# Elementwise work of the projections from GpSimd to VectorE, and layer 1's first in-projection spread over the whole second output stage

## The chip, the cores and the metric

The kernel runs on one core of a Trainium2 chip. The metric is device time in microseconds (us), lower is better. The kernel before takes 3068.93 us, the median of three runs (3067.5 to 3072.47). Engines go by the profile's names: PE is TensorE's matmul, PEld its weight load, DVE is VectorE, ACT is ScalarE, POOL is GpSimd, SP is SyncE, which issues all DMAs here.

## The reference, cut to what matters

A decoder trunk of two layers over 1040 tokens of width 1024 (16 meta tokens in front of 1024), in float32:

```python
for layer in range(2):
    hn = rmsnorm(h, norm_mix_w[layer])
    hq,hf,hi,hg, gq,gk,gv,gz, ga,gb, su = split(hn @ w_in[layer])   # 1024 x 3336
    y_a = hgrn2_mixer(hq, hf, hi, hg, ...)      # 4 heads of 64, chunked recurrence
    y_b = gdn_mixer(gq, gk, gv, gz, ga, gb, ...)  # conv + silu, 4 heads of 128, triangular solve per chunk, state
    y_c = s5_mixer(su, ...)                     # 16 groups, linear state space, gelu, gate
    h = h + concat(y_a, y_b, y_c) @ w_out[layer]      # 1024 x 1024
    hn = rmsnorm(h, norm_mlp_w[layer])
    h = h + square(relu(hn @ w1[layer])) @ w2[layer]  # 1024 x 4096 x 1024
return rmsnorm(h, final_norm_w)[:, 16:]
```

The recurrences carry a state from one token chunk to the next.

## The kernel before

The 1040 tokens are two blocks of 520, b = 0 and 1, with the width on the partitions (eight tiles of 128 x 520). For each layer and block there are three parts: the in-projection (`projection`), the recurrences over the block (`states`), and the output stage (`out_mlp`: w_out, norm, MLP).

**Weights.** Every product with w_in, w_out, w1 or w2 is done in split precision: the operand x as xh + xl, the weight as wh + wl, three matmuls for each. A weight tile is a "granule" of 128 x 512 (four 128 x 128 pieces): SP loads it to `wr`, ACT makes the high part `wh` (line 459), and the low part `wl` is a tensor_tensor at line 113, called from `split`. There are three buffers each of wr, wh and wl (N_W). A granule feeds 24 matmuls of 260 to 264 columns, or 12 of 512. A product with w_in, w_out or w1 takes two granules, one with w2 takes one. Products go to two PSUM buffers `pd`; DVE takes them out.

**In-projection.** 26 products with w_in and a narrow one, in this order: S5's inputs, rows of gates (`in_rows`), convolutions for the delta-net heads with SiLU (`in_conv`, `silu`), between them the decay matrices (`gdn_decay`), a triangular solve (`gdn_solve`), in block 0 the tables of S5 (`s5_layer`), more convolutions, gates (`in_gate`), and the two pairs of HGRN heads (`in_hgrn`, then `hgrn`: many small matmuls in `mxh`, exponentials, products).

**States.** `states` runs the delta-net windows (ten items, each a chain of a dozen steps, the state `GS` handed on from window to window) beside S5. Their matmuls write `mxt`, and each item ends in a DMA at line 1043 that stores its outputs `ydr`. The output stage of a block reads all of that block's ydr first.

**Order.** `run` writes: in-projection and states of (layer 0, b 0), the same of (0, 1), output stage of (0, 0); then layer 1's first in-projection interleaved with output stage (0, 1); then states (1, 0); then the rest of output stage (0, 1); in-projection and states of (1, 1); output stages (1, 0) and (1, 1). In the interleaved part each piece of the projection allows so many units of the output stage, one unit being one granule's product: DENSE after a product, MIX after a step of decay or HGRN. A list scheduler then orders the instructions of each engine, weights ahead of the rest; what is written late can stand early on an engine, but within one engine the order is fixed when the program runs.

Lines 107, 110, 113, 116, 121 and 125 are helpers, so in the profile tile names tell the work apart: `pd` products, `s` rows of 520 in the projection, `h` the residual, `uh`/`ul` the MLP's hidden operand, `mh`/`nh`/`qh` projection scratch, `mt`/`nt` states scratch.

Of the kernel before, what the change touches and what calls it, by code (L numbers as in the profile page):

```python
# [94 lines left out]
class Kern:  # L95
# [91 lines left out]
    def setup(self):  # L187

        nc = self.nc
        self.take(T)  # L190
        self.K, self.XD, self.SC, self.grp = {}, None, None, "h"
        warm = self.n([128, 2, 128])
        nc.vector.memset(warm, 0.0)
        for _ in range(7):
            self.mm(self.mps()[:, :256], warm[:, 0], warm.rearrange("p a b -> p (a b)"))
        self.ident = self.load_const("ident", [128, 128])
        nc.scalar.preload_act_table_set("natural_log_exp_and_others")
# [269 lines left out]
    def granule_now(self, fill, keep):  # L467
        raw = self.tl(self.big, [128, 4, 128], "wr", N_W)
        fill(raw)
        if keep:  # L470
            lo, hi = [self.operand(tag)[:, :512].rearrange("p (k m) -> p k m", k=4) for tag in ("xl", "xh")]
        else:
            lo = self.tl(self.big, [128, 4, 128], "wl", N_W, F32R)
            hi = self.tl(self.big, [128, 4, 128], "wh", N_W, F32R)
        self.split(raw, hi, lo, self.nc.gpsimd)
        return hi, lo

    def weights(self, ap):
# [30 lines left out]
    def normed_rows(self, h, wcol, b, spare=None):  # L509

        nc = self.nc
        xs = [], []
        acc = self.s()
        for k in range(KD):
            self.square(acc, h[k], k)
        self.squares, self.r = acc, None
        r = self.scale()
        if b == 0:
            self.hist = self.tl(self.big, [128, KD, HIST], "hist", 1)
        for k in range(KD):  # L520
            w = self.prm[:, wcol + k:wcol + k + 1]
            xn = self.tl(self.sp, [128, T + 8], "s", N_S)[:, :T + HIST]
            if b == 0:
                nc.gpsimd.memset(xn[:, :HIST], 0.0)
            else:
                nc.gpsimd.tensor_copy(xn[:, :HIST], self.hist[:, k])
            self.stt(xn[:, HIST:], h[k], w, r, ALU.mult, ALU.mult)
            if b == 0:
                nc.gpsimd.tensor_copy(self.hist[:, k], xn[:, T:])
            hi, lo = (next(spare), next(spare)) if spare else (self.operand("xh"), self.operand("xl"))  # L530
            nc.scalar.copy(hi, xn)
            self.tt(lo, xn, hi.bitcast(F32), ALU.subtract)
            xs[0].append(hi)
            xs[1].append(lo)
        return xs
# [45 lines left out]

    def silu(self, n, out):
        self.sigma(out, n)
        self.tt(out, out, n, ALU.mult, eng=self.nc.gpsimd)

    def cols(self, l, col, xs, runs=None):
        wts = self.ready.pop((l, col), None) or self.in_weights(l, col)
# [5 lines left out]
    def cols_ab(self, l, xs):  # L593


        nc = self.nc
        wi = self.ins["w_in"][l].rearrange("(g k p) m -> g p k m", k=4, p=128)
        ps = self.tl(self.pd, [128, 2, 512], "pd", 2)
        for g in range(2):
            raw = self.tl(self.big, [128, 4, 128], "wr", N_W)[:, :, :8]  # L600
            w = self.tl(self.big, [128, 4, 128], "wh", N_W, F32R)
            nc.sync.dma_start(raw, wi[g][:, :, C_GA:C_GA + 8])
            nc.scalar.copy(w[:, :, 0:32].rearrange("p k (r m) -> p k r m", r=4), raw.unsqueeze(2).to_broadcast([128, 4, 4, 8]))
            self.tt(w[:, :, 32:40], raw, w[:, :, 0:8].bitcast(F32), ALU.subtract, eng=nc.gpsimd)
            for k in range(4 * g, 4 * g + 4):
                for c in range(2):
                    cs = slice(HIST + c * HN, HIST + (c + 1) * HN)
                    self.mm(ps[0:40, c, :HN], w[:, k % 4, 0:40], xs[0][k][:, cs], start=(k == 0), stop=False)
                    self.mm(ps[0:40, c, :HN], w[:, k % 4, 0:40], xs[1][k][:, cs], start=False, stop=(k == KD - 1))
        return ps  # L610
# [118 lines left out]
    def projection(self, l, b, xs, hook=None, first=False):  # L729


        DENSE, MIX = 2, 0.5
        self.Y = self.YS[b] = self.tl(self.dr, [KD, 128, T], "ydr", 2)
        if first:
            self.setup_mixers()
        g = {"z": self.tl(self.dr, [6, 128, T], "gated", 2)}
        us = self.in_s5(l, xs)
        yield 2 * DENSE
        g["rows"] = self.in_rows(l, b, xs)
        yield MIX  # L740
        g["qkv"] = self.QKV = self.tl(self.dr, [12, 128, T], "qkvd", 2)
        self.gdn_begin(l, b, g)
        for p in range(2):
            for i in (2 * p, 2 * p + 1, 4 + 2 * p, 5 + 2 * p):
                self.in_conv(l, b, xs, i)
                yield DENSE
            for _ in pipeline([self.gdn_decay(g, w, p) for w in range(NW)], GAP_DECAY):
                yield MIX
        self.gdn_solve()
        self.gdn_scales()  # L750
        if b == 0:
            self.s5_layer(l)
        if hook:
            trace(hook)
        for i in range(8, 12):
            self.in_conv(l, b, xs, i)
            yield DENSE
        for i in range(4):
            self.in_gate(l, xs, C_GZ + 128 * i, g["z"][i])
            yield DENSE  # L760
        for j in range(2):
            hd = self.in_hgrn(l, xs, j)
            yield 3 * DENSE
            self.in_gate(l, xs, C_HG + 128 * j, g["z"][4 + j])
            yield DENSE
            for _ in self.hgrn(l, b, j, hd, g["z"][4 + j]):
                yield MIX
        self.mixed = g, us
# [82 lines left out]
    def gdn_decay(self, g, w, pair):  # L851
# [23 lines left out]
        self.act(ln, ln, AF.Ln, bias=EPS)  # L875
        self.act(b2, ln, AF.Exp, scale=-1.0)
        MA = self.m()[:W, :4 * W].rearrange("p (a b c) -> p a b c", a=2, b=2)
        self.tt(MA, E.unsqueeze(1).to_broadcast([W, 2, 2, W]), K["tri"].unsqueeze(2).to_broadcast([W, 2, 2, W]), ALU.mult, eng=nc.gpsimd)
        self.tt(b2, b2, self.gsc[:, w, 1, hs], ALU.mult)
        yield  # L880
        self.tt(MA[:, 0], MA[:, 0], b2.unsqueeze(2).to_broadcast([W, 2, W]), ALU.mult, eng=nc.gpsimd)
        self.tt(MA, pg, MA, ALU.mult)
        yield
        nc.sync.dma_start(self.item(self.MAd, it), MA)
# [15 lines left out]
    def gdn_solve(self):  # L900
# [20 lines left out]
        low = lambda t: t[:, H:, 0:H]  # L921
        mid = self.n([80, H, H])
        for dst, a, bt in ((mid, low(Dg), Tm[:, 0:H, 0:H]), (low(Tm), Tm[:, H:, H:], mid)):
            for n, i0 in enumerate(range(0, H, 3)):
                k = min(3, H - i0)
                prod = tmp()[:, :k * H * H].rearrange("p (i c j) -> p i c j", i=k, c=H)
                self.tt(prod, bt.rearrange("p j c -> p c j").unsqueeze(1).to_broadcast([80, k, H, H]),
                        a[:, i0:i0 + k, :].unsqueeze(2).to_broadcast([80, k, H, H]), ALU.mult, eng=nc.gpsimd if n % 2 else None)
                nc.vector.tensor_reduce(dst[:, i0:i0 + k, :], prod, mybir.AxisListType.X, ALU.add)
        Tt = Dg  # L930
        nc.scalar.copy(Tt, Tm.rearrange("p a b -> p b a"))
# [373 lines left out]
    def out_mlp(self, l, b, h, last=False):  # L1305
# [10 lines left out]
        for m in range(KD):  # L1316
            ps = self.product(self.weights(self.ins["w_out"][l][:, 128 * m:128 * m + 128]), xs)
            self.tt(self.half(h[m]), self.half(h[m]), ps, ALU.add)
            yield 2
        xs = self.normed(h, 16 + 8 * l)  # L1320
        NG = D_FF // 512
        hid = {}
# [140 lines left out]
    def run(self):  # L1463
        self.setup()
        self.H, self.YS = {}, {}
        nxt = {}

        def early():

            nxt[1] = self.htiles()  # L1470
            yield from self.load_x(1, nxt[1])
            self.save_h(1, nxt[1])
        h = self.htiles()
        trace(self.load_x(0, h))
        self.ready = {(0, col): self.in_weights(0, col) for col in (C_SU, C_SU + 128)}
        self.setup_norms()
        self.block(0, 0, h, early(), True)
        self.block(0, 1, nxt[1])
        h = self.get_h(0)
        trace(self.out_mlp(0, 0, h))  # L1480
        xs = self.normed_rows(h, 8, 0, self.spare_operands())
        self.save_h(0, h)

        h = self.get_h(1)
        rest = self.out_mlp(0, 1, h)
        due = 0
        for n in self.projection(1, 0, xs):
            due += n
            while due > 0:
                due -= next(rest, 1e6)  # L1490
        self.states(1, 0)
        trace(rest)
        self.save_h(1, h)
        self.block(1, 1, h)
        for b in range(NB):

            self.take(512 if b == 0 else T)
            h = self.get_h(b)
            self.steps = None
            trace(self.out_mlp(1, b, h, b == 1))  # L1500
            self.finish(b, h, self.steps)


# [27 lines left out]
```

## Time and profile before

| | |
|---|---|
| median of three runs | 3068.93 us |
| the profiled execution's own time, its span | 3072.88 us, 3071.1 us |
| mean granted TensorE clock | 0.954 of 2.4 GHz |
| busy, share of the span | PE 93%, PEld 87%, DVE 51%, ACT 42%, POOL 51% |
| chain that ended last, by engine | PE 68%, DVE 13%, DMA 5% |

The stretches in which the rows below are cut follow the issue of each part's first weights: 26 to 264 us is the in-projection of (0, 0); 264 to 568 that of (0, 1) with states (0, 0); 568 to 1132 output stage (0, 0); 1132 to 1894 output stage (0, 1), with layer 1's first in-projection up to about 1645 and states (1, 0) behind it; 1894 to 2106 the in-projection of (1, 1); 2106 to 2613 output stage (1, 0) with states (1, 1); then output stage (1, 1). What overlaps is cut by its start.

A busy time is a union of spans. PE counts as busy also while it works at the lower of its two clock levels, 1.2 GHz, so a stretch's clock is to be read beside it.

### The profile page before, as it was taken

The page shows a single profiled execution, that of the slowest core. Times are in us where ns is not written, and L with a number is a line of the kernel's source. Part 1 is how long each engine was busy: PE and PEld are TensorE (multiplying, and loading weights), DVE is VectorE, ACT ScalarE, POOL GpSimd, SP SyncE. Part 2 cuts the span into 40 slices and gives each one's busy share as a digit, 9 for nine tenths or more (in the row PEclk, how much of TensorE's full clock was granted, in tenths as well). Part 3 has the DMA queues.
Part 4 walks back from the last instruction along what each step waited for, and adds up shares of the span by engine and source line. Part 5 has one row for each costly group of instructions (what it writes and reads, how often), then busy time and mean ns, then how long its engine had stood idle before and what let it go on. Part 6 is the DMA issues. An engine that isn't in the chain of part 4 may idle for free.

```text
span 3071.1 us, 60499 instructions
## 1 busy us (share of the span) xinstructions
PE 2844.3 (93%) x23513; PEld 2658.8 (87%) x23513; DVE 1571.5 (51%) x2905; ACT 1302.2 (42%) x2657; POOL 1581.0 (51%) x1425
## 2 busy tenths in 40 slices
PE   7777999979999998987999998988999999999998
PEld 6776889969899998987998998987877788999998
DVE  7588764775532234668535434577554322522224
ACT  4534455534443334533443434454544333433332
POOL 4555475764634445564656344577364444444443
PEclk8897899989999999998998999998999999999999
DMA  5755555744433344445544444565444333533332
GB/s 147 192 125 162 150 153 135 209 86 119 120 90 102 92 132 115 126 112 123 153 117 118 123 128 135 140 165 136 132 122 108 99 94 98 161 90 92 92 93 80
DMA packets 641611, 381.18 MB, mean 124 GB/s; under 512 B 166239, under 2 KB 599237, under 8 KB 641325
## 3 DMA queue, kind: packets, MB, share of 16 engines
q1 hardware_dynamic: 641325, 377.31, 44.8%
q8 instruction: 186, 3.05, 0.4%
q14 instruction: 100, 0.82, 0.1%
HBM read 308.52 MB, written 70.43 MB: 123 GB/s over the span
## 4 chain that ended last, share of the span: by engine, by line
PE 68%; DVE 13%; DMA 5%; issue 2%; ACT 2%; POOL 1%; SPq 0%; DVEq 0%; POOLq 0%; ACTq 0%
PE pd L125 57%; PE mxt L125 7%; DVE mh L113 4%; PE mxh L125 2%; DVE s L116 2%; DVE s L113 1%; DMA nt<-rowd 1%; ACT s L110 1%; DMA ys<-ydr 1%; DVE s L648 1%; DVE mt L113 0%; DVE nh L113 0%; DMA nh<-rowd 0%; DVE s L121 0%; DVE h L113 0%
## 5 line engine op out<-in xcount | busy, mean ns | idle before, releaser
L113 POOL TENSOR_TENSOR wl<-wr,wh 128x512 fp32r<-128x512 f32 x776 | 1023.4, 1321 | 1073.4 <-ACT wh L459 999.5
L459 ACT CAST wh<-wr 128x512 fp32r<-128x512 f32 x776 | 478.2, 617 | 887.2 <-PE pd L125 753.6
L125 PE MATMUL pd<-xh,wh 128*128 128x260 f32 (+3 forms) x3256 | 744.0, 301 | 47.6 <-DVE s L116 12.9
L125 PE MATMUL pd<-xl,wh 128*128 128x260 f32 (+3 forms) x3256 | 741.7, 300 | 6.8 <-DVE xl L113 4.7
L125 PE MATMUL pd<-xh,wl 128*128 128x260 f32 (+2 forms) x3208 | 729.7, 300 | 4.3 <-POOL wl L113 4.1
L125 PEld LDWEIGHTS pd<-xh,wh 128*128 128x128 f32 x3256 | 526.2, 192 | 67.3 <-issue 25.1
L125 PEld LDWEIGHTS pd<-xl,wh 128*128 128x128 f32 x3256 | 528.3, 193 | 22.7 <-DVE xl L113 5.8
L125 PEld LDWEIGHTS pd<-xh,wl 128*128 128x128 f32 x3208 | 520.5, 193 | 20.3 <-POOL wl L113 5.8
L125 PE MATMUL pd<-uh,wh 128*128 128x260 f32 (+1 forms) x2008 | 474.2, 304 | 16.9 <-DVE h L113 13.3
L125 PE MATMUL pd<-uh,wl 128*128 128x260 f32 (+1 forms) x2008 | 472.3, 304 | 0.5 <-POOL wl L113 0.5
L125 PE MATMUL pd<-ul,wh 128*128 128x260 f32 (+1 forms) x2008 | 472.5, 303 | 0.0
L113 DVE TENSOR_TENSOR h<-h,pd 128x520 f32<-128x520 f32 (+2 forms) x296 | 200.4, 678 | 379.3 <-PE pd L125 377.4
L110 ACT ACTIVATE s<-s 128x520 f32<-128x520 f32 (+3 forms) x431 | 272.0, 635 | 212.1 <-DVE s L121 146.3
L125 PEld LDWEIGHTS pd<-uh,wh 128*128 128x128 f32 x2008 | 324.7, 191 | 33.0 <-issue 15.4
L125 PEld LDWEIGHTS pd<-uh,wl 128*128 128x128 f32 x2008 | 324.1, 190 | 13.9 <-POOL wl L113 0.7
L125 PEld LDWEIGHTS pd<-ul,wh 128*128 128x128 f32 x2008 | 324.2, 190 | 13.7 <-issue 0.4
L116 DVE SCALAR_TENSOR_TENSOR s<-pd,r 128x520 f32<-128x520 f32 (+2 forms) x121 | 83.7, 692 | 280.1 <-PE pd L125 279.9
L113 DVE TENSOR_TENSOR ul<-s,uh 128x520 fp32r<-128x520 f32 (+1 forms) x129 | 100.5, 780 | 130.9 <-ACT uh L459 130.6
L113 POOL TENSOR_TENSOR s<-s 128x520 f32<-128x520 f32 x80 | 111.6, 1395 | 88.3 <-ACT s L110 67.1
L116 DVE SCALAR_TENSOR_TENSOR s<-pd,cvw,s 128x520 f32<-128x520 f32 x144 | 108.5, 754 | 65.4 <-ACT s L110 63.7
L125 PE MATMUL pd<-mt,wh 128*128 128x264 f32 (+3 forms) x594 | 106.0, 299 | 20.0 <-DVE s L116 7.7
L113 DVE TENSOR_TENSOR s<-s 128x520 f32<-128x520 f32 (+3 forms) x119 | 106.8, 902 | 26.6 <-ACT s L110 24.1
(274 smaller groups left out, 3646.9 us busy)
## 6 DMA issues: line engine op xcount, KB each, us to landing
wr<-in_mlp_w_dram SPq DMA_DIRECT2D x512, 256.0 KB
wr<-in_w_in_dram SPq DMA_DIRECT2D x208, 256.0 KB
wr<-in_w_out_dram SPq DMA_DIRECT2D x64, 256.0 KB
qkvd<-s SPq DMA_DIRECT2D x48, 260.0 KB
win<-qkvd SPq DMA_DIRECT2D x40, 312.0 KB
hdr<-h SPq DMA_DIRECT2D x32, 260.0 KB
mh<-qkvd SPq DMA_DIRECT2D x40, 208.0 KB
hd<-s SPq DMA_DIRECT2D x32, 260.0 KB
```

What stands on the lines that cost most here:

```text
L110: return self.nc.scalar.activation(out, in_, func, **kw)
L113: return (eng or self.nc.vector).tensor_tensor(out, a, b, op)
L116: return self.nc.vector.scalar_tensor_tensor(out, a, s, b, op0, op1)
L125: return self.nc.tensor.matmul(out, lhsT, rhs, start=start, stop=stop, **kw)
L459: self.nc.scalar.copy(hi, src)
L648: self.nc.vector.tensor_tensor_scan(out[:, ws], self.K["ones"][:n, 0:1].to_broadcast([n, W]), x[:, ws], 0.0, ALU.mult, ALU.add)
```

## The change

`self.low` is a new field that names the engine for a granule's low part: None, which `tt` takes as VectorE, at the start; GpSimd from the MLP of an output stage on, other than that of (layer 0, b 1); None again after output stage (0, 0) and before each `finish`. Counted over the program, 408 of 784 low parts are on VectorE after, and all 784 were on GpSimd. SiLU's 80 multiplications, two of each `gdn_decay` (40 items), 16 of `gdn_solve` and eight small ones of `cols_ab` go to VectorE too, and 32 copies of four columns from GpSimd to ScalarE. In the interleaved part DENSE goes from 2 to 2.5 and MIX from 0.5 to 1, and `states(1, 0)` is written behind the end of output stage (0, 1).

```diff
@@ setup
+        self.low = None
@@ granule_now
-        self.split(raw, hi, lo, self.nc.gpsimd)
+        self.split(raw, hi, lo, self.low)
@@ normed_rows
-                nc.gpsimd.tensor_copy(xn[:, :HIST], self.hist[:, k])
+                nc.scalar.copy(xn[:, :HIST], self.hist[:, k])
...
@@ silu
-        self.tt(out, out, n, ALU.mult, eng=self.nc.gpsimd)
+        self.tt(out, out, n, ALU.mult)
@@ projection
-        DENSE, MIX = 2, 0.5
+        DENSE, MIX = 2.5, 1
@@ gdn_decay
-        self.tt(MA, E.unsqueeze(1)..., K["tri"]..., ALU.mult, eng=nc.gpsimd)
+        self.tt(MA, E.unsqueeze(1)..., K["tri"]..., ALU.mult)
...
-        self.tt(MA[:, 0], MA[:, 0], b2..., ALU.mult, eng=nc.gpsimd)
+        self.tt(MA[:, 0], MA[:, 0], b2..., ALU.mult)
@@ gdn_solve
-                        a[:, i0:i0 + k, :]..., ALU.mult, eng=nc.gpsimd if n % 2 else None)
+                        a[:, i0:i0 + k, :]..., ALU.mult)
@@ out_mlp, behind the products with w_out
+        if l or b == 0:
+            self.low = nc.gpsimd
@@ run
         trace(self.out_mlp(0, 0, h))
+        self.low = None
...
-        self.states(1, 0)
         trace(rest)
         self.save_h(1, h)
+        self.states(1, 0)
         self.block(1, 1, h)
...
             trace(self.out_mlp(1, b, h, b == 1))
+            self.low = None
             self.finish(b, h, self.steps)
```

On VectorE, in the interleaved part, a convolution stands beside the first products of the MLP (`s<-pd,cvw,s` is a tap of the convolution, `s<-pd,r` takes a hidden product out of PSUM, `ul<-s,uh` is its low part). Before:

```order
L116 SCALAR_TENSOR_TENSOR s<-pd,cvw,s 128x520 x3
L113 TENSOR_TENSOR mh<-mxt,mh 104x416
L121 TENSOR_SCALAR s<-s 128x520
L116 SCALAR_TENSOR_TENSOR s<-pd,r 128x520
L113 TENSOR_TENSOR ul<-s,uh 128x520
L116 SCALAR_TENSOR_TENSOR s<-pd,cvw,s 128x520 x3
```

The same place after:

```order
L113 TENSOR_TENSOR wl<-wr,wh 128x512 x2
L116 SCALAR_TENSOR_TENSOR s<-pd,cvw,s 128x520 x3
L113 TENSOR_TENSOR wl<-wr,wh 128x512
L121 TENSOR_SCALAR s<-s 128x520
L116 SCALAR_TENSOR_TENSOR s<-pd,r 128x520
L113 TENSOR_TENSOR wl<-wr,wh 128x512
L113 TENSOR_TENSOR s<-s 128x520
L113 TENSOR_TENSOR ul<-s,uh 128x520
L113 TENSOR_TENSOR h<-h,pd 128x520
```

The low parts of weights, and SiLU's `s<-s`, now stand in one queue with the rows that take products out of PSUM.

On PE, in the in-projection of (1, 1), where the convolutions' products (264 columns) give way to the gates' (260). Before:

```order
L125 MATMUL pd<-xl,wh 128x264 x2
L125 MATMUL pd<-xh,wl 128x264 x2
L125 MATMUL pd<-xh,wh 128x260 x2
L125 MATMUL pd<-xl,wh 128x260 x2
L125 MATMUL mxt<-mh 104x104 x4
L125 MATMUL pd<-xh,wl 128x260 x2
```

After, shortly ahead of the same switch (`GS` is the delta-net state, `win` a window of q, k and v):

```order
L125 MATMUL pd<-xl,wh 128x264
L125 MATMUL mxt<-nt 52x52 x2
L125 MATMUL mxt<-GS,win 104x128 x2
L963 MATMUL mxt<-ident,win 104x128
L964 MATMUL mxt<-ident,win 104x128
L963 MATMUL mxt<-ident,win 104x128
L964 MATMUL mxt<-ident,win 104x128
L125 MATMUL pd<-xl,wh 128x264
L125 MATMUL pd<-xh,wl 128x264 x2
```

States (1, 0), which before stood among the MLP's products, stand after among the products of the in-projection of (1, 1).

## Rows read from the trace of the kernel before

**Rows 1.** The page: the span and each engine's busy time.

```profile
span 3071.1 us, 60499 instructions
PE 2844.3 (93%) x23513; PEld 2658.8 (87%) x23513; DVE 1571.5 (51%) x2905; ACT 1302.2 (42%) x2657; POOL 1581.0 (51%) x1425
```

**Rows 2.** Stretches: busy us (count) of PE, PEld, DVE, ACT, POOL; clock, DMA share, GB/s.

```profile
26.00:264.00 238.00, 181.75 (x1360) 172.59 (x1358) 189.14 (x424) 105.76 (x229) 125.88 (x106) 0.89 0.58 148
264.00:568.00 304.00, 277.43 (x2746) 255.95 (x2747) 190.06 (x372) 163.67 (x376) 184.16 (x186) 0.92 0.58 157
568.00:1132.00 564.00, 533.14 (x4900) 514.22 (x4900) 263.48 (x475) 220.35 (x460) 286.87 (x265) 0.96 0.41 110
1132.00:1470.00 338.00, 293.55 (x2316) 288.27 (x2316) 225.01 (x410) 145.51 (x280) 179.31 (x150) 0.93 0.47 126
1470.00:1645.00 175.00, 173.32 (x1722) 167.38 (x1722) 69.76 (x117) 76.27 (x143) 101.18 (x90) 1.00 0.44 129
1645.00:1894.00 249.00, 242.86 (x2239) 229.03 (x2238) 112.94 (x234) 100.55 (x227) 116.07 (x120) 0.95 0.44 120
1894.00:2106.00 212.00, 184.09 (x1420) 180.56 (x1419) 139.34 (x217) 107.08 (x218) 129.31 (x110) 0.93 0.62 160
2106.00:2613.00 507.00, 499.85 (x3157) 402.48 (x3155) 218.29 (x383) 208.72 (x420) 260.34 (x241) 0.99 0.38 109
```

**Rows 3.** The same, of `pd` alone: PE, PEld, DVE, ACT.

```profile
925.00:1127.00 202.00, 202.00 (x1681) 201.94 (x1679) 35.90 (x52) 0.00 (x0) 1.00 0.33 96
1645.00:1894.00 249.00, 175.24 (x1259) 160.19 (x1258) 27.05 (x39) 0.00 (x0) 0.95 0.44 120
```

**Rows 4.** The same, of HGRN's `mxh` (first row) and of the states' `mxt` (second).

```profile
1645.00:1894.00 249.00, 16.46 (x408) 11.88 (x408) 7.25 (x24) 5.43 (x19) 0.95 0.44 120
...
1645.00:1894.00 249.00, 76.38 (x572) 63.22 (x572) 32.02 (x90) 17.25 (x56) 0.95 0.44 120
```

**Rows 5.** SP in order of time: first and last store of states (1, 0).

```profile
1706.58 0.53 SPq L1043 DMA_DIRECT2D ydr<-nt  x1
...
1890.09 0.37 SPq L1043 DMA_DIRECT2D ydr<-nt  x1
```

**Rows 6.** Groups by line and form, POOL: busy us, mean ns, idle before, releaser.

```profile
L113 POOL TENSOR_TENSOR wl<-wr,wh 128x512 fp32r<-128x512 f32 x776 | 1023.4, 1321 | 1073.4 <-ACT wh L459 999.5 <-PE pd L125 32.7 <-DMA wr<-in_mlp_w_dram 6.9
L113 POOL TENSOR_TENSOR s<-s 128x520 f32<-128x520 f32 x80 | 111.6, 1395 | 88.3 <-ACT s L110 67.1 <-DVE mh L113 15.1 <-DVE Tm L920 5.2
```

**Rows 7.** One line's rows on DVE by tile: duration ns min/median/max.

```profile
L113 DVE TENSOR_TENSOR ul<-s,uh x129: 414/701/1780, 678.7 to 3033.0; 128x520 fp32r<-128x520 f32 x95, 128x512 fp32r<-128x512 f32 x32, 128x260 fp32r<-128x260 f32 x2
L121 DVE TENSOR_SCALAR s<-s x64: 408/430/2199, 57.2 to 2116.2; 128x520 f32<-128x520 f32 x52, 4x520 f32<-4x520 f32 x8, 8x520 f32<-8x520 f32 x4
...
L113 DVE TENSOR_TENSOR h<-h,pd x296: 418/695/699, 588.1 to 3059.2; 128x520 f32<-128x520 f32 x104, 128x512 f32<-128x512 f32 x36, 128x260 f32<-128x260 f32 x8
...
L113 DVE TENSOR_TENSOR gsc<-gsc x44: 127/180/2287, 107.5 to 2038.6; 104x2 f32<-104x2 f32 x40, 104x20 f32<-104x20 f32 x4
```

**Rows 8.** Groups by line and form, DVE, for two lines of rows 7.

```profile
L121 DVE TENSOR_SCALAR s<-s 128x520 f32<-128x520 f32 x52 | 36.8, 709 | 0.9
...
L113 DVE TENSOR_TENSOR gsc<-gsc 104x2 f32<-104x2 f32 x40 | 22.8, 571 | 2.2 <-ACT gsc L110 2.2
```

**Rows 9.** DVE and POOL in order of time, 1238 to 1250 us.

```profile
1241.23 2.35 DVE L116 SCALAR_TENSOR_TENSOR s<-pd,cvw,s 128x520 f32<-128x520 f32 x3 [6.30 <-ACT s L110]
1243.61 1.48 DVE L121 TENSOR_SCALAR s<-s 128x520 f32<-128x520 f32 x1
...
1243.52 1.29 POOL L113 TENSOR_TENSOR wl<-wr,wh 128x512 fp32r<-128x512 f32 x1 [1.62 <-ACT wh L459]
```

**Rows 10.** Who waited for whom: total us, times, longest.

```profile
ACT wh L459 <- PE pd L125: 753.6, 447, 4.5
DVE ul L113 <- ACT uh L459: 133.3, 102, 2.3
DVE s L116 <- ACT s L110: 63.7, 28, 6.3
```

More of the change, by code (lines that the diff above doesn't have):

```diff
@@ L525, in normed_rows @@
             else:
-                nc.gpsimd.tensor_copy(xn[:, :HIST], self.hist[:, k])
+                nc.scalar.copy(xn[:, :HIST], self.hist[:, k])
             self.stt(xn[:, HIST:], h[k], w, r, ALU.mult, ALU.mult)
             if b == 0:
-                nc.gpsimd.tensor_copy(self.hist[:, k], xn[:, T:])
+                nc.scalar.copy(self.hist[:, k], xn[:, T:])
             hi, lo = (next(spare), next(spare)) if spare else (self.operand("xh"), self.operand("xl"))
@@ L603, in cols_ab @@
             nc.scalar.copy(w[:, :, 0:32].rearrange("p k (r m) -> p k r m", r=4), raw.unsqueeze(2).to_broadcast([128, 4, 4, 8]))
-            self.tt(w[:, :, 32:40], raw, w[:, :, 0:8].bitcast(F32), ALU.subtract, eng=nc.gpsimd)
+            self.tt(w[:, :, 32:40], raw, w[:, :, 0:8].bitcast(F32), ALU.subtract)
             for k in range(4 * g, 4 * g + 4):
@@ L877, in gdn_decay @@
         MA = self.m()[:W, :4 * W].rearrange("p (a b c) -> p a b c", a=2, b=2)
-        self.tt(MA, E.unsqueeze(1).to_broadcast([W, 2, 2, W]), K["tri"].unsqueeze(2).to_broadcast([W, 2, 2, W]), ALU.mult, eng=nc.gpsimd)
+        self.tt(MA, E.unsqueeze(1).to_broadcast([W, 2, 2, W]), K["tri"].unsqueeze(2).to_broadcast([W, 2, 2, W]), ALU.mult)
         self.tt(b2, b2, self.gsc[:, w, 1, hs], ALU.mult)
         yield
-        self.tt(MA[:, 0], MA[:, 0], b2.unsqueeze(2).to_broadcast([W, 2, W]), ALU.mult, eng=nc.gpsimd)
+        self.tt(MA[:, 0], MA[:, 0], b2.unsqueeze(2).to_broadcast([W, 2, W]), ALU.mult)
         self.tt(MA, pg, MA, ALU.mult)
@@ L923, in gdn_solve @@
         for dst, a, bt in ((mid, low(Dg), Tm[:, 0:H, 0:H]), (low(Tm), Tm[:, H:, H:], mid)):
-            for n, i0 in enumerate(range(0, H, 3)):
+            for i0 in range(0, H, 3):
                 k = min(3, H - i0)
@@ L927, in gdn_solve @@
                 self.tt(prod, bt.rearrange("p j c -> p c j").unsqueeze(1).to_broadcast([80, k, H, H]),
-                        a[:, i0:i0 + k, :].unsqueeze(2).to_broadcast([80, k, H, H]), ALU.mult, eng=nc.gpsimd if n % 2 else None)
+                        a[:, i0:i0 + k, :].unsqueeze(2).to_broadcast([80, k, H, H]), ALU.mult)
                 nc.vector.tensor_reduce(dst[:, i0:i0 + k, :], prod, mybir.AxisListType.X, ALU.add)
```

## The prediction

> **What bounds the kernel now.** I read the page's engine rows first: PE is busy 2844.3 of 3071.1 us, all others at about half [rows 1]. So PE's work is the floor, and only what PE does not do at full pace can be won: 227 us in which it is not busy, and the part of its busy time at the lower clock.
>
> The view by stretch then says where that is [rows 2]. From 2106 to 2613 us PE is busy 499.85 of 507 at a clock of 0.99, so nothing is to be had there. The gaps lie in the in-projections: 56 us from 26 to 264 (clock 0.89), 27 from 264 to 568, 31 in the output stage of (0, 0), 44 from 1132 to 1470 (0.93), 28 from 1894 to 2106 (0.93). A clock of 0.93 over 184 busy us costs up to 13 us more, over 293.55 up to 21. In just these stretches DVE is fullest: 189 of 238, 225 of 338, 139 of 212 us, against 218 of 507 later. PE waits there for a chain through VectorE, and has nothing else to do.
>
> What PE can do when fed: 1681 products in 202 us at full clock, 0.120 us each [rows 3].
>
> **The states behind the stage, and the denser spread.** This moves PE's work from a place without holes to places with holes. In 1645 to 1894 us the rest of the MLP runs beside states (1, 0): 1259 products, at 0.120 us 151 us [rows 3]; HGRN's tail, 16 us; and the states' own matmuls, at most 76 us of busy PE [rows 4].
>
> After, the MLP products go forward, into the interleaved part: by the code the projection's 26 dense and 71 mixed allowances let 26 x 2 + 71 x 0.5 = 87.5 of the stage's 144 units through before, and 26 x 2.5 + 71 = 136 now. I price that part as its present 513 us (1132 to 1645) plus 151 plus 16, less what the new products fill. The holes on offer are 44 us and 21 of clock between 1132 and 1470 [rows 2]. Those lie around the solve and S5's tables, long runs on VectorE, and VectorE gets more work too, so I take a quarter, 16 us. Bounds: 0 (VectorE decides there) and 65 (all filled). So 664 us.
>
> The in-projection of (1, 1) takes the states in: 212 + 76 = 288 us, less the filled holes. On offer are 28 us and 13 of clock. I take 30; bounds 0 and 41. So 258 us. Two floors speak for a value in this region. The states of (1, 0) took 183.5 us from first store to last, 1706.58 to 1890.09, beside a dense PE [rows 5], and a head start of the first item comes on top, so a stage that holds the chain isn't much below 220. And the stretch from 264 to 568 is the same mixture in layer 0 with both HGRN pairs in it: 304 us, PE busy 277 of them [rows 2].
>
> Sum: 664 + 258 = 922, against 1132 to 2106, 974 us: 52 us less. Behind it, output stage (1, 0) reads ydr of states (1, 0), which before were long there; now it can start only when they end. In my sum they end with the in-projection, so I add nothing; if the chain ends 20 us later, PE has only the small matmuls of HGRN (1, 1) meanwhile, and most of the 20 would be lost.
>
> **VectorE instead of GpSimd.** A low part costs GpSimd 1.32 us, a SiLU product 1.40 [rows 6]. VectorE's row of the same kind, `ul<-s,uh`, has a median of 0.70 us [rows 7]. The added instructions per in-projection are 52 low parts, 20 SiLU products, 20 in decay, 4 in the solve and 2 narrow ones, 98; at 0.70 us at most 69 us (the decay's are narrower; the solve's wider in steps, so this is an estimate). Four times that is 276. Output stage (0, 1) adds 144 low parts, 101 us; w_out of the other three stages and the last eight, 56, 39 us. In all some 416 us on a VectorE that is busy 1571.5.
>
> Against this stands what VectorE gets back. Its rows that read PSUM don't vary: `h<-h,pd` has a median of 0.695 and a maximum of 0.699 us. Its rows out of SBUF do: a `gsc` of two columns takes from 0.127 to 2.287 us, the TENSOR_SCALAR on `s` from 0.408 to 2.199 [rows 7]. In order of time such a row, 1.48 us long, starts within 0.1 us of a low part of 1.29 us on GpSimd [rows 9]. The two groups lose 36.8 - 52 x 0.430 = 14 us and 22.8 - 40 x 0.180 = 16 us, 40% and 68% of their time [rows 7, 8]. GpSimd's busy time falls by 408 x 1.32 + 80 x 1.40 = 651 of 1581 us at least, and most of that where VectorE is full. How much comes back in all I can only bound: at least the 30 us of these groups times that share, about 12, and at most the 416 that is added.
>
> The Trainium skill has two rules that pull apart here. SBUF — State Buffer, "Who interferes with whom", says that a VectorE instruction with two SBUF inputs contends with a GpSimd instruction that reads SBUF; the rows just told agree (0.70 us at the median, 1.78 at most for `ul`, none for PSUM). By it nearly all that is lost would come back with GpSimd's rows gone. Perfetto Trace Analysis, "Optimizing Scalar/DVE Operations", says that with a saturated VectorE, work may well be handed to ScalarE or even GpSimd; by that the change goes the wrong way in the fullest stretch, and its time is rival C below. The same section grants that handing work between these two might not help, as they share a port.
>
> On the path: from 264 to 568 VectorE with 69 us more has 259 of 304, still room. From 26 to 264 it would have 258 of 238 if nothing came back, 20 us too many; if half of the added time came back, 224, which fits. So there the term lies between +20 and, with the 56 us of holes partly caused by held VectorE rows, -30. In the other stages VectorE has room. I take 0 for the whole, bounds -60 (a half of the 114 us of holes before 1132 goes) and +70 (two in-projections lose 20, and 30 low parts come a microsecond late). The 32 copies on ScalarE are of four columns and lie beside ScalarE's idle half.
>
> **Sum.** 3072.88 - 52 + 0 = 3021 us against the profiled execution; the median of runs shown is 4 us below that one, so 3017 us.
>
> **Rivals.** *B, both pay in full.* The holes of the interleaved part and of the last in-projection fill (65 + 41 instead of 16 + 30, 60 us more), or half of that and layer 0 gains 30 too. For it: VectorE's held time sits where PE waits. Against: what remains in the interleaved part is the solve and S5's tables, which are chains and not throughput. Time 2957 to 2985, about 2965.
>
> *C, VectorE is the bound in the holes.* Nothing comes back, so the spread finds VectorE full: no hole is filled (46 us of the 52 go) and the first stretch loses 20. For it: 79% busy from 26 to 264. Against: rows held to many times their length [rows 7]. Time 3017 + 46 + 20 = 3083, or 3068 if only half of the 20 and of the missing fill comes with some payback elsewhere.
>
> *D, the low parts wait in VectorE's queue: slower.* On GpSimd a low part waited for `wh` alone. On VectorE it stands behind rows that wait for ScalarE: a convolution's tap waited 6.30 us in one place [rows 9], the MLP's `ul` 102 times 1.3 us [rows 10]. `wh` itself follows PE's release of a buffer (753.6 us of waiting) [rows 10], and with three buffers two granules, 5.8 us, lie ahead of PE; less 0.70 for the low part and, as an estimate, as much for the cast, some 4.4 us of slack. If 80 of the 400 come late by 1.3 us, 104 us are lost: 3017 + 104 = 3121. It outweighs the gain from 40 late ones. Against it: the 28 waits of the taps sum to 63.7 us, 2.3 each, and the 102 of `ul` are 1.3, so few are longer than the slack; and the new order puts low parts ahead of the taps in the place shown.
>
> That the change doesn't do what it says can be left aside for the order: the states do stand among the last in-projection's products.
>
> **How the numbers follow.** Forecast 0.50, B 0.22, C 0.12, D 0.16. The forecast's own range, 2985 to 3050, is all faster; C is half within 0.2% (6 us, about what a measurement of this kernel can tell from no change) and half slower; of D 0.14 is slower, 0.01 the same and 0.01 faster. Faster 0.50 + 0.22 + 0.01 = 0.73, same 0.06 + 0.01 = 0.07, slower 0.06 + 0.14 = 0.20. The range from 2960 to 3100 leaves out B's lower part (0.10) and D's upper (0.10).
>
> **What would show it.** In the changed profile: states' `ydr` stores of (1, 0) lie beside the in-projection of (1, 1), whose part takes about 258 us with PE busy over 95%; the interleaved part takes about 664 us and holds all products of output stage (0, 1); VectorE's maximum on `gsc` and on the TENSOR_SCALAR falls where low parts are on VectorE; VectorE's busy time lies between 1.6 and 1.9 ms and GpSimd's near 0.9 ms. I would be wrong if PE's waits named `wl` on DVE by tens of us (D), if the first 264 us grew (C), or if output stage (1, 0) began with a hole while the states end.

## The result and the profile after

The changed kernel takes 2988.09 us, the median of four runs (2985.49 to 2990.42), against 3070.7 (3067.5 to 3074.94) for the kernel before on the same chip: ratio 0.973, 95% interval 0.9713 to 0.9747, 83 us less. The forecast was 3017, its own range 2985 to 3050; the time lies 3 us inside its lower end.

The page of the changed kernel: span, busy time by engine, and the two groups of low parts (busy, mean ns, idle before, releaser).

```profile
span 2986.0 us, 60325 instructions
PE 2815.6 (94%) x23513; PEld 2632.9 (88%) x23513; DVE 1702.9 (57%) x3497; ACT 1309.7 (44%) x2689; POOL 820.5 (27%) x801
...
L113 DVE TENSOR_TENSOR wl<-wr,wh 128x512 fp32r<-128x512 f32 x400 | 282.0, 705 | 106.2 <-ACT wh L460 101.6
...
L113 POOL TENSOR_TENSOR wl<-wr,wh 128x512 fp32r<-128x512 f32 x376 | 494.2, 1315 | 720.6 <-ACT wh L460 663.1
```

Against [rows 1] PE is busy 28.7 us less and idle 56.4 less (170.4 instead of 226.8). DVE has 592 more instructions and is busy 131.4 us more; POOL's busy time has halved. A low part costs 0.705 us on VectorE and 1.315 on GpSimd.

The changed kernel by stretch (length, then busy us and count of PE, PEld, DVE, ACT, POOL, then clock, DMA share, GB/s), each cut where a part's first weights are issued:

```profile
26.00:237.20 211.20, 177.67 (x1323) 171.41 (x1324) 168.48 (x460) 105.64 (x231) 0.95 (x5) 0.87 0.62 162
237.20:517.60 280.40, 252.35 (x2599) 234.19 (x2598) 216.50 (x458) 154.85 (x339) 81.08 (x90) 0.94 0.57 156
517.60:1093.80 576.20, 551.11 (x5090) 527.88 (x5090) 279.79 (x563) 234.27 (x511) 251.44 (x236) 0.97 0.43 117
1093.80:1747.40 653.60, 627.39 (x5700) 613.45 (x5699) 426.78 (x857) 285.28 (x539) 48.61 (x68) 0.98 0.45 124
1747.40:1984.40 237.00, 227.98 (x1842) 217.41 (x1841) 167.49 (x324) 130.40 (x284) 34.87 (x40) 0.96 0.62 170
1984.40:2531.30 546.90, 521.73 (x3316) 420.69 (x3315) 273.37 (x534) 226.36 (x482) 243.16 (x228) 0.98 0.43 116
2531.30:2986.00 454.70, 442.74 (x3599) 438.02 (x3598) 156.82 (x257) 160.88 (x271) 157.48 (x122) 0.99 0.34 101
```

For the comparison, the three stretches in which the order works, of the kernel before, cut at the same marks:

```profile
1132.40:1897.00 764.60, 712.32 (x6291) 687.28 (x6291) 409.31 (x761) 323.59 (x651) 397.75 (x360) 0.95 0.46 125
1897.00:2106.10 209.10, 181.19 (x1396) 177.66 (x1395) 137.48 (x215) 105.92 (x217) 127.82 (x109) 0.93 0.61 159
2106.10:2615.70 509.60, 502.44 (x3170) 404.64 (x3169) 219.96 (x385) 209.87 (x422) 261.63 (x242) 0.99 0.38 109
```

Here and below, A is the interleaved part, B the in-projection of (1, 1), C output stage (1, 0). A fell by 111.0 us, B grew by 27.9 and C by 37.3. Layer 0's two in-projections fell by 26.9 and 24.0; its output stage rose by 12.3, which is work that came over from the part ahead (5090 matmuls, before 4900 [rows 2]). C was full before (502.44 of 509.6); it now has 18.0 us more idle PE and 19.3 us more busy PE, with 146 more matmuls. A and B together have 145 fewer, so this work came over from them.

### The profile page after: what moved, and what is told of

It reads as the page before. It is cut to its first block, busy times and chain, and to the rows that moved or that the text cites. A ratio compares the mean times of both kernels' runs of the same rounds, so it can differ in the third digit from the quotient of the medians.

```text
span 2986.0 us, 60325 instructions
## 1 busy us (share of the span) xinstructions
PE 2815.6 (94%) x23513; PEld 2632.9 (88%) x23513; DVE 1702.9 (57%) x3497; ACT 1309.7 (44%) x2689; POOL 820.5 (27%) x801
## 4 chain that ended last, share of the span: by engine, by line
PE 78%; DVE 10%; DMA 7%; issue 2%; ACT 1%; POOL 1%; SPq 0%; DVEq 0%; ACTq 0%; POOLq 0%
PE pd L125 66%; PE mxt L125 8%; DVE mh L113 3%; PE mxh L125 3%; DVE wl L113 1%; DVE s L116 1%; DVE s L113 1%; DMA nh<-rowd 1%; DMA XD<-diag 1%; DMA ys<-ydr 1%; DVE mt L113 1%; DMA mh<-qkvd 0%; DMA mh<-rowd 0%; DVE h L113 0%; POOL mh L113 0%
## 5 line engine op out<-in xcount | busy, mean ns | idle before, releaser
L125 PE MATMUL pd<-xh,wl 128*128 128x260 f32 (+2 forms) x3208 | 719.4, 297 | 2.7 <-POOL wl L113 1.7
L113 POOL TENSOR_TENSOR wl<-wr,wh 128x512 fp32r<-128x512 f32 x376 | 494.2, 1315 | 720.6 <-ACT wh L460 663.1
L125 PEld LDWEIGHTS pd<-xl,wh 128*128 128x128 f32 x3256 | 522.1, 191 | 19.9 <-DVE xl L113 3.0
L113 DVE TENSOR_TENSOR wl<-wr,wh 128x512 fp32r<-128x512 f32 x400 | 282.0, 705 | 106.2 <-ACT wh L460 101.6
L113 DVE TENSOR_TENSOR s<-s 128x520 f32<-128x520 f32 (+3 forms) x199 | 137.8, 696 | 54.9 <-ACT s L110 53.4
L113 DVE TENSOR_TENSOR ul<-s,uh 128x520 fp32r<-128x520 f32 (+1 forms) x129 | 93.8, 729 | 114.6 <-ACT uh L460 114.0
L113 POOL TENSOR_TENSOR nt<-nt 128x208 f32<-128x208 f32 x80 | 54.2, 678 | 367.1 <-ACT nt L110 247.7
```

Source lines behind the costliest of these rows:

```text
L113: return (eng or self.nc.vector).tensor_tensor(out, a, b, op)
L125: return self.nc.tensor.matmul(out, lhsT, rhs, start=start, stop=stop, **kw)
```

## The experiments

Lengths by stretch in us, from the profiles of the four kernels that separate the two halves; "engines" is all that moves between engines, "order" is DENSE, MIX and the place of the states:

| part | before | order alone | engines alone | both (the change) |
|---|---|---|---|---|
| in-projection (0, 0) | 238.1 | 238.9 | 211.7 | 211.2 |
| in-projection (0, 1), states (0, 0) | 304.4 | 304.1 | 281.2 | 280.4 |
| output stage (0, 0) | 563.9 | 566.5 | 577.2 | 576.2 |
| A, interleaved part | 764.6 | 684.6 | 736.8 | 653.6 |
| B, in-projection (1, 1) | 209.1 | 237.8 | 206.6 | 237.0 |
| C, output stage (1, 0) | 509.6 | 543.4 | 513.2 | 546.9 |
| output stage (1, 1), end | 455.4 | 454.9 | 454.5 | 454.7 |

**Engines alone.** The changed kernel with the order of before.

```diff
-        DENSE, MIX = 2.5, 1
+        DENSE, MIX = 2, 0.5
+        self.states(1, 0)
         trace(rest)
         self.save_h(1, h)
-        self.states(1, 0)
```

> The engine moves alone, order as before (DENSE 2, MIX 0.5, states (1, 0) in their old place). Theory V (VectorE gains its held time back): layer 0 is then as in the changed kernel, some 39 us earlier at the first weights of layer 1, and layer 1's two in-projections gain a little as well: about 3015 us. Rival O (only the order pays, VectorE breaks even): 3065 to 3075 us.

3008.66 us, ratio 0.9805 [0.9782, 0.9827]: 60.9 us less than before, three quarters of the whole. Of 63.9 us between the spans 36.3 come from layer 0 and 26.7 from A, B and C.

**Order alone.** The kernel before with the opposite edit.

> The order alone (DENSE 2.5, MIX 1, states (1, 0) behind output stage (0, 1)), all on GpSimd as before. Theory: layer 1 gains on its own, 46 us if the two edits are independent: about 3025 us, layer 0 as before. Rival (the denser spread needs a VectorE that is not held): no gain or slower, 3060 to 3090 us, with PE's waits for VectorE grown between 1132 and 1900 us.

3058.16 us, 0.9964 [0.9952, 0.9975]: 11.4 us less. That is 2 us below the rival's 3060 to 3090 and far from the theory's 3025. A and B give 51.3, C takes 33.8 back. On top of the engines (the table's last two columns) it is 52.8 and 33.7, 20.6 us by the medians. C grows alike with either engine, so VectorE's new load isn't what lengthens it.

**The low parts alone, and the rest alone** (order of before in both). The first gives the kernel before only `self.low`; the second takes from engines alone just that:

```diff
-        self.split(raw, hi, lo, self.low)
+        self.split(raw, hi, lo, self.nc.gpsimd)
```

> Only the weights' low parts go to VectorE where the change puts them; SiLU, decay, solve and the small copies stay on GpSimd, order as before. If the low parts' hold on VectorE is what costs (they are 539 of some 760 us taken off GpSimd), this has most of the gain of the engine moves, about 3025 us. Rival (the latency of SiLU and of decay, 1.4 against 0.7 us in a chain, is what pays): 3055 us or more.

3014.01 us, 0.9829 [0.9809, 0.9849], 55.5 less.

> The other half: SiLU, decay, solve, narrow ones and copies moved, the weights' low parts on GpSimd, order as before. By the low parts theory 3055 to 3065 us; by the latency rival about 3025 us.

3046.34 us, 0.9938 [0.992, 0.9956], 23.2 less, between the two expectations: the low parts are most of the gain but not all. Together the two would be 79; both at once gave 61, so they overlap.

**The states written early again, and the spread sparse again.** Each undoes one part of the order in the changed kernel.

```diff
+        self.states(1, 0)
         trace(rest)
         self.save_h(1, h)
-        self.states(1, 0)
```

> The changed kernel with states (1, 0) written where they were, before the rest of output stage (0, 1); the engine moves and the spread (2.5 and 1) stay, so only 8 units, some 23 us, are left behind them. Theory T: the changed order wins 50 us up to output stage (1, 0) and gives 34 us back there, because its products wait for the chain of states (1, 0). An earlier start of the chain gives part of that back: 2965 to 2980 us, stage (1, 0) shorter than 547 us. Rival: the two orders come to the same, 2988 us, since the chain stands beside the same in-projection; or slower (3000 us) since the states hold up the last 8 units and so the norm of block 1.

2977.95 us, 0.9695 [0.9679, 0.9711]: 10 us faster than the changed kernel. A is 7.9 us longer (661.5), C 16.9 shorter (530.0):

```profile
1992.00:2522.00 530.00, 515.06 (x3231) 414.96 (x3230) 253.27 (x500) 218.60 (x455) 242.22 (x224) 0.97 0.42 114
```

```diff
-        DENSE, MIX = 2.5, 1
+        DENSE, MIX = 2, 0.5
```

> The changed kernel with DENSE 2 and MIX 0.5 as before; states (1, 0) stay behind the stage. If the place of the states alone makes the order's gain, this is as fast as the changed kernel, 2985 to 2992 us. If the denser spread is needed too (56 more units of the stage, 161 us of products, to fill the projection's holes), the rest of the stage runs after it in one dense piece and the holes of the interleaved part stay: 3005 to 3020 us.

3000.24 us, 0.9773 [0.9758, 0.9788], between the two expectations. A is 672.6, B 239.1, C 538.1. Thus from engines alone (3008.66) the denser spread by itself gives 31 us (to 2977.95), the states' move by itself 8 (to 3000.24; these two intervals overlap), and both 21 (to 2988.09): with the dense spread the move costs 10.

**GpSimd reads, or only writes, beside VectorE.** At each low part that is on VectorE, GpSimd gets extra work that nobody uses. The first is four subtractions of 64 columns of a constant, the second twelve fills of 64 columns:

```diff
+        if self.low is None and "ones" in self.K:
+            junk, one = self.tl(self.big, [128, 64], "junk", 1), self.K["ones"][:, :64]
+            for _ in range(4):
+                self.tt(junk, one, one, ALU.subtract, eng=self.nc.gpsimd)
```

```diff
...
+            for _ in range(12):
+                self.nc.gpsimd.memset(junk, 0.0)
```

> The changed kernel and, beside each low part on VectorE, four GpSimd subtractions of 128x64 that read a constant and write a scratch that nobody reads or waits for, about 1.3 us of GpSimd together, as long as the low part that it replaces. Theory V (GpSimd's reads hold VectorE's): VectorE's rows out of SBUF get long maxima again (the two-column gsc over 1 us), its busy time rises by 60 us or more, and the time by 20 to 45 us, to 3010 to 3030 us. Rival (GpSimd was only too slow in the chain): nobody waits for it here, so 2988 us within 8.

3083.55 us, 1.0043 [1.0028, 1.0058], 95 us above the changed kernel, but not for the reason expected. Durations of `gsc` on VectorE (min/median/max ns), and GpSimd in order of time (start, us):

```profile
L113 DVE TENSOR_TENSOR gsc<-gsc x44: 144/155/268, 115.7 to 2146.8; 104x2 f32<-104x2 f32 x40, 104x20 f32<-104x20 f32 x4
```

```profile
199.63 82.78 POOL L113 TENSOR_TENSOR junk<-ones 128x64 f32<-128x64 f32 x166
282.54 0.53 POOL L403 MEMSET mh<- 128x512 f32 x1
```

These rows are nearly undisturbed (0.268 us at most), and VectorE is busy 1725.0 us, 22 more than in the changed kernel. But 166 idle subtractions stand in GpSimd's queue ahead of a fill that S5's tables need, and PE waited for `mh` 35.6 us in two waits (10.3 in the changed kernel); another 110 stand ahead of a low part for which PE waited 20.0 us. The run measures mainly a clogged queue, not a held VectorE: these waits are some 45 of the 95 us, and the rest was not traced.

> The same with twelve GpSimd memsets of 128x64 in place of the subtractions: GpSimd is about as busy, but reads nothing. Theory V (it is the reading that holds VectorE): VectorE's rows stay as in the changed kernel and the time within 8 us of 2988. If any work of GpSimd on SBUF holds VectorE, as the run with reads, 3010 us or more.

2996.32 us, 0.9764 [0.9749, 0.9779], 8 us above the changed kernel. GpSimd fills for 748.2 us, `gsc` takes 0.175 us at most, and VectorE is busy 1706.4 us, 3.5 more: these fills hold it hardly at all.

**Each low part computed twice**, on VectorE and once more on GpSimd into scratch: the full-size read. One of the three buffers `ys` had to go for the scratch, so the same with that buffer alone gone is the control.

```diff
+        if self.low is None:
+            junk = self.tl(self.big, [128, 4, 128], "junk", 1)
+            self.tt(junk, raw, hi.bitcast(F32), ALU.subtract, eng=self.nc.gpsimd)
```

> The changed kernel in which GpSimd computes each of VectorE's low parts a second time, 128x512 from the same two inputs, into a scratch that nothing reads; one buffer of the output operand is given up for the scratch (its own cost is measured by the next kernel). So GpSimd's wide reads of before are back and VectorE keeps its work. Theory V (wide GpSimd reads hold VectorE's rows): the two-column gsc is over 1 us at its longest again, VectorE's busy time is 60 us or more above the changed kernel's 1703, and the time 20 to 60 us longer than without the scratch. Rival (what paid is the shorter way through the chain, 0.7 for 1.3 us, and VectorE was never held): maxima as in the changed kernel and the time within 8 us of the next one.

> The changed kernel with two buffers in place of three for the output operand's loads, the control for the scratch: 2988 to 2998 us by either theory.

The control takes 2989.66 us (0.9735 [0.9718, 0.9753]), no cost. With the second reading it is 3130.25, 1.0191 [1.0171, 1.0211], 141 us above the control, more than twice the upper end of what was expected. Its page and the `gsc` rows:

```profile
PE 2862.3 (91%) x23513; PEld 2666.3 (85%) x23513; DVE 1967.8 (63%) x3497; ACT 1304.2 (42%) x2689; POOL 1457.1 (47%) x1209
...
L113 POOL TENSOR_TENSOR junk<-wr,wh 128x512 f32<-128x512 f32 x400 | 621.9, 1555 | 808.2 <-ACT wh L460 625.2 <-issue 82.6 <-DMA h<-hdr 31.2
L113 DVE TENSOR_TENSOR gsc<-gsc x44: 141/148/1297, 114.8 to 2188.3; 104x2 f32<-104x2 f32 x40, 104x20 f32<-104x20 f32 x4
```

The same 3497 instructions keep VectorE busy 1967.8 instead of 1702.9 us, 265 more, and a two-column `gsc` again takes up to 1.297. What this doesn't separate in the time: GpSimd's reading also holds `wr` and `wh` longer.

The fills were as narrow as the subtractions that hardly held VectorE, so by these three runs it could be the width of GpSimd's rows, and not their reading. A count over all fourteen traces tells the two apart. It takes VectorE's tensor_tensors with both inputs in SBUF and compares each with the fast rows of its own line, tiles and form in the same run (their 20th percentile):

| what alone GpSimd runs beside the row | rows | longer by, mean ns | at most, ns |
|---|---|---|---|
| nothing | 14497 | 4 | 119 |
| fills of 200 or more columns | 94 | 5 | 20 |
| tensor_tensors of 64 columns | 539 | 40 | 158 |
| tensor_tensors of 200 or more columns | 4281 | 349 | 4058 |

VectorE's rows that read PSUM are longer by 3 ns beside wide tensor_tensors (7300 rows) and by 4 beside nothing. So wide fills hold nobody, and wide tensor_tensors, which read, do.

**All low parts on VectorE, and the two best edits together.** The first changes `self.low = nc.gpsimd` in `out_mlp` to `None`; the second has that and the states early.

> The changed kernel with the low parts of all output stages on VectorE too (376 more, some 263 us). Theory V: VectorE is never held by a low part, also not in the HGRN and states work beside output stages (0, 0) and (1, 0), where PE has some 50 us of holes: 2965 to 2985 us. Rival (VectorE's queue: low parts wait behind rows that wait for PE or ScalarE): 2995 us or more, with PE's waits for wl on VectorE grown.

2977.39 us, 0.9688 [0.9665, 0.9711], 11 below the changed kernel. 376 more low parts at 0.705 us are 265 us; DVE is busy 201 more (1904.2). PE waits for `wl` on VectorE 9.5 us in all.

> The changed kernel with both edits that were faster than it: states (1, 0) written before the last 8 units of output stage (0, 1), and all low parts on VectorE. If the two gains (10 us from the earlier chain in output stage (1, 0), 11 us from an unheld VectorE in the output stages) come from different places, they add: 2962 to 2970 us. If both fill the same hole at the start of output stage (1, 0): 2973 to 2980 us.

2963.93 us, 0.9662 [0.9641, 0.9684], the fastest version here: the two gains add up.

## Why the prediction was right, and which steps were not

The time lay in the forecast's own range by two errors of opposite sign: VectorE's part was priced 0 and gave 61, and output stage (1, 0) was priced 0 and took back 34. That they cancel so far is luck.

**A and B: right as a sum, by luck in part.** The forecast was 664 + 258 = 922 us; order alone has 684.6 + 237.8 = 922.4. A came 20 us longer than worked out and B 20 shorter, and B is shorter also because some of its work now lies in C. In the changed kernel B's PE is busy 227.98 of 237 us, 96%, as forecast. That a stage that holds the chain isn't much below 220 held too.

**The mis-sized term: "In my sum they end with the in-projection, so I add nothing."** The states don't end with it. SP of the changed kernel in order of time:

```profile
1801.58 0.41 SPq L1044 DMA_DIRECT2D ydr<-nt  x1
...
1984.38 0.37 SPq L482 DMA_DIRECT2D wr<-in_w_out_dram  x1
...
2010.25 0.36 SPq L1044 DMA_DIRECT2D ydr<-nt  x1
```

The first and last store are 208.7 us apart (183.5 before [rows 5]), and the last comes 26 us behind the stage's first weights. So the hole that the prediction feared is there. PE of the changed kernel in order of time:

```profile
2014.29 1.41 PE L125 MATMUL mxt<-mh 128*104 128x104 f32 x8 [4.57 <-DVE mh L113]
...
2021.38 1.22 PE L125 MATMUL pd<-uh,wh 128*128 128x512 f32 x2 [2.21 <-ACT uh L460]
```

The products with w_out that need the last outputs start at 2021.38, 11 us behind the last store; until then PE has only matmuls of the decay and waits 8.6 us in three waits. This isn't the whole loss. With the states early the last store is at 1979.3, 13 us ahead of C's first weights, PE waits for nothing up to 2030, and C is still 20 us longer than before. VectorE of the changed kernel in order of time, at the end of the states:

```profile
1992.15 0.60 DVE L116 SCALAR_TENSOR_TENSOR nt<-mxt,gsc,mt 104x128 f32<-104x128 f32 x2
...
1995.10 0.17 DVE L828 COPY gsc<-gtok 104x20 f32<-104x20 f32 x1
```

The first row is the last read of `gsc` by states (1, 0), the second VectorE's first write of `gsc` for block (1, 1); ScalarE's first one starts within 0.1 us of it. `gsc` has one buffer (`"gsc", 1`, as `gtok`, `gln` and `diag`). The decay matrices of (1, 1) need it, so they can't be finished until the states of (1, 0) are done, and behind them stand the triangular solve and HGRN. In six kernels whose states run beside the last in-projection the write follows the last read by 0.3 to 2.7 us. Its input isn't what it waits for: `gtok` was complete at 1842.9 in the changed kernel, 152 us ahead. In the kernel before, the last read was at 1875.9 and the write at 1971.7, free of each other, and just behind `gtok` (1971.5). The solve's last reductions, changed kernel and before (in front of the shapes: first and last start):

```profile
L930 DVE TENSOR_REDUCE Tm<-mh x5: 306/659/660, 2093.2 to 2096.7; 80x39 f32<-80x507 f32 x4, 80x13 f32<-80x169 f32 x1
```

```profile
L929 DVE TENSOR_REDUCE Tm<-mh x5: 315/667/671, 2075.3 to 2080.7; 80x39 f32<-80x507 f32 x4, 80x13 f32<-80x169 f32 x1
```

Before, the solve ended 25 us ahead of C's start (2106.1); now it ends 112 us inside C (1984.4). While C's norm runs, PE now lacks the 340 small matmuls of HGRN that came from 2128.9 to 2186.4 before, and gets them from 2127.9 to 2179.7, 143 us behind the start instead of 23. PE's other waits in C of the changed kernel, 15.1 us in seven, lie there, from 2070 to 2115. The three longest:

```profile
2098.11 0.47 PE L125 MATMUL pd<-xh,wh 128*128 128x512 f32 x1 [2.51 <-DVE s L116]
2109.08 0.47 PE L125 MATMUL pd<-uh,wh 128*128 128x512 f32 x1 [2.70 <-DVE s L116]
2114.60 0.92 PE L125 MATMUL mxt<-mt,D 128*64 128x65 f32 x12 [4.82 <-DMA mt<-ud]
```

In the first two PE waits for VectorE to take a product out of PSUM, which it does at 2097.30, right behind the solve, and at 2108.26, behind eight rows of the projection (`mh<-qh`, 7.64 us together). The third is a load of S5's inputs for states (1, 1).

| kernel | write of `gsc` against C's first weights, us | C, us |
|---|---|---|
| before; engines alone | -134; -134 | 509.6; 513.2 |
| states early; the same, all low parts on VectorE | -28; -28 | 530.0; 519.2 |
| order alone; sparse; all low parts on VectorE | +2; +2; +3 | 543.4; 538.1; 537 |
| changed | +11 | 546.9 |

C grows with the lateness of that write. That the single buffer is the cause is read from this order; no kernel with two buffers was run, so it isn't shown by an experiment. Nor is it shown that two of `gsc` would be enough: `MAd`, which the states read (last at 1957.0) and the decay writes, has one buffer too.

**VectorE's part: sign within the bounds, size at the far one.** The bounds were -60 and +70, and I took 0 between them; it came to -61. The failed step is "how much comes back in all I can only bound". By the estimate 416 us of work went to VectorE; it is busy 131 us more, so some 285 came back, not the 12 that the two groups shown made sure of. Summed over both traces by form, the rows that VectorE had before are 215 us shorter, and the added ones take 406; the rest is overlap of neighbouring rows, since a busy time is a union. The total lies in the 1.6 to 1.9 ms named, and the two groups do as forecast. The changed kernel by tile and by form:

```profile
L113 DVE TENSOR_TENSOR gsc<-gsc x44: 151/155/187, 107.2 to 2054.7; 104x2 f32<-104x2 f32 x40, 104x20 f32<-104x20 f32 x4
L121 DVE TENSOR_SCALAR s<-s 128x520 f32<-128x520 f32 x52 | 22.9, 441 | 0.2
```

187 ns at most instead of 2287 [rows 7], and 22.9 us instead of 36.8 [rows 8]. The second reading (265 us more on VectorE), the fills (3.5) and the count over the traces show that GpSimd's wide rows that read SBUF hold VectorE's rows with SBUF inputs. How much of the 61 us is this, and how much the shorter way through the chain (a low part takes 0.705 for 1.315 us), no run separates.

The Trainium skill, SBUF — State Buffer, "Who interferes with whom", says of such rows: a VectorE instruction with two SBUF inputs contends with GpSimd's reads, not with its writes. The count (349 ns beside wide reading rows, 5 beside wide fills) and the runs with 512 columns (1.297 us) and with fills (0.175) agree; the one with 64 columns (0.268) hardly shows it. The other rule that was weighed, Perfetto Trace Analysis, "Optimizing Scalar/DVE Operations", to hand work away from a full VectorE (which it hedges for GpSimd), points the other way, and this case does not bear it out: VectorE was busy 189 of 238 us in the first stretch [rows 2], was given more, and is busy 168 of 211.

**The rivals.** C (VectorE is the bound) falls with that stretch: shorter by 27 us where it asked for 20 more. D (low parts wait in VectorE's queue) falls by one row, PE's waits for low parts on VectorE in the changed kernel:

```profile
PE pd L125 <- DVE wl L113: 1.0, 1, 1.0
```

B (both pay in full, 2965) was nearest in mechanism: the engines paid in full, but the holes did not all fill, and C gave back.

**What was not asked: which half of the order pays.** The prediction priced the spread and the states' place as one. The runs part them: the spread gives 31 us, and moving the states on top of it costs 10, since after 136 of 144 units little of the stage is left for them to run beside (A 7.9 us shorter), while each microsecond by which they end later is a later write of `gsc`.

## What to carry to other kernels

When a chain is moved under the next part's products, ask when its outputs are due, and look past them to its single-buffered inputs: the next part's own chain may wait for their release, and the cost then appears a stage later, in a place that was full. When GpSimd's wide two-input rows lie beside VectorE rows whose longest is many times their shortest, price the move to VectorE by the stretched rows and not by the busy share. Split a change of two parts by a run of each before believing that a right sum had right terms.

## What the runs showed of the hardware

Not expected: how much the width of GpSimd's reads matters. 1616 subtractions of 64 columns (0.411 us each, 664.4 us in all) left VectorE's `gsc` at 0.268 us at most, while 400 of 512 columns (1.555 us each, 621.9 us) took it to 1.297. Over all traces a row of VectorE with two SBUF inputs is longer by 40 ns beside the narrow ones and by 349 beside wide ones. Why the narrow ones hold VectorE so little is open; in the two runs they also differ in what they read (one small constant, or freshly loaded weights) and in when they run.
